# Stores whose tile ScalarE wrote last, issued from ScalarE's own transfer queue

## The chip, the cores and the metric

The kernel runs on one core of a Trainium2 chip. The metric is the device time of one execution in microseconds (us). The engines are TensorE (PE, with its weight loads as PEld), VectorE (DVE), ScalarE (ACT), GpSimd (POOL) and SyncE (SP); a "q" behind a name (SPq, ACTq) means the engine's sequencer, which waits and issues transfers.

## The reference

One layer of a streaming encoder with two parallel token mixers, on 2048 tokens of width 1024, in float32:

```
xn = RMSNorm(x)
[aq|ak|av|mq|mk|mv|mo|i|f|ga|gm] = xn @ w_in
A = chunked band attention (8 heads of 64, own chunk of 64 + 8 before, learned position bias)
M = mLSTM matrix memory (4 heads of 128, chunkwise; causal conv on q/k; headwise RMSNorm; sigmoid(mo))
y = sigmoid(ga) * (A @ w_att_proj) + sigmoid(gm) * (M @ w_mlstm_proj)
x = x + y @ w_out
x = x + relu(RMSNorm(x) @ w_up)^2 @ w_down
out = RMSNorm(x)
```

## The kernel before, in words

**Data.** The tokens are four blocks (b = 0 to 3) of 512. A tile is 128 partitions by 512 columns of float32 (256 KB). On-chip memory holds small pools of such tiles: 16 `ctx`, 6 `temp` (named tmp in the profile), 4 `sc`, 28 `r` (two halves each), 4 `wraw` and 3 `wsp` for weights, and 8 PSUM banks. Everything that is needed later is stored to DRAM and loaded again: gates (`gate`), conv outputs and output gates (`mfar`), values (`vspill`, `mvfar`), keys and queries (`kfar`, `qfar`), the ungated feed-forward activations (`u`), partial sums (`park`), combined weights (`wsum`).

**Products.** A float32 product is done as three passes over a high and a low half: ScalarE casts a tile to the high half, VectorE subtracts for the low half (weights: `split_now`, L501 and L503; operands: `split`, L1109 and L1114, L1111 and L1116), and PE runs high x high, high x low, low x high. Large products are done on 2 x 2 blocks with seven block products instead of eight (`quad`, L631; `product`, L662), so sums of blocks are made by VectorE and stored or split. `copied` (L1790) and `summed` (L1798) take results out of PSUM on ScalarE and VectorE.

**Stages.** In order: values for blocks 0 and 1; the input products (gates through tanh at L1930, the output gate `mo` scaled again at L1936); input products of blocks 2 and 3 with attention and recurrence of blocks 0 and 1 woven between; the projections of the mixers; the output product; the feed-forward up product, whose result is made relu (L2119) and square (L2123) by ScalarE; the down product, for the first half with attention and recurrence of blocks 2 and 3 woven in; the second half's out, up and down; the final norm.

**The order.** The program is written out by a planner, `Flow`. Every piece of work is a generator, a thread, that asks for an engine with a time (`yield "act", ns`), for a tile of a pool, or waits for an event. `Flow.run` always takes the request with the earliest planned start, advances the planned clock of that engine, and lets the thread emit its instructions. `fl.now` is the planned time of the running thread and the engine that set it. A request may hold two numbers: the first books the engine, the second is added for the thread alone. A transfer is a request for "sp": 800 ns of booked time for 256 KB, 1570 ns for 512 KB, and 2000 ns until it has landed. PE takes instructions in the order that the planner chose.

**Transfers.** All transfers but five are issued by SP. The five of ScalarE are a 12 KB load at the start (L308) and four stores of the output at the end (`turned_put`, L2316). Most stores go through one helper, `store`, L2041, whose issue is L2043. It is called by `sum_w` (weights), `park_u2` and `park_v`, `merge` (with the queue "sp!"), `evac_v` and `evac_mv` (values; the latter's writer is ScalarE at L1567), `gates_kept` and `gates_rest` (ScalarE at L1391 and L1521), `take_x1`, `keep` (the seven blocks of `u`), `after_vm`, `parts` (queries and keys: one half written by ScalarE at L1907, the other by VectorE at L1909), `after_in` (gates), `conv_far`, `x2_tile`, `norm_mid`, `final_keep` and `table`. For `u`, `sums` sends the blocks a11 and a12 directly when their square is done, and a22 and a21 behind VectorE steps:

```
yield "wait", [evs["a11"]]
a11 = tiles["a11"][:, :512]
send(0, a11)
```

Of the kernel before, what the change touches and what calls it, by code (L numbers as in the profile page):

```python
# [101 lines left out]
class Flow:  # L102
# [10 lines left out]
               act=dict(pe=220.0, act=130.0, dve=130.0, pool=180.0),  # L113
               dve=dict(pe=220.0, act=130.0, dve=130.0, pool=155.0), pool=dict(pe=290.0, act=130.0, dve=60.0),
               sp=dict())
# [132 lines left out]
class Layer:  # L248
# [1790 lines left out]
        fl.put(self.ctx, x)  # L2039

    def store(self, dst, src, ev, pool=None, item=None, queue="sp"):  # L2041
        yield queue, 800, 2000
        self.nc.sync.dma_start(dst, src)  # L2043
        self.fl.set(ev)
        if pool is not None:
            self.fl.put(pool, item)
# [517 lines left out]
```

## Time and profile before

| | |
|---|---|
| time, median of 3 runs | 2753.01 us (2751.06 to 2756.75) |
| profiled execution, its own time | 2753.07 us |
| its span | 2751.3 us |
| instructions | 38074 |
| granted PE clock | 0.998 |
| DMA: bytes, mean rate | 673.57 MB, 245 GB/s |
| issued from SP's queue (q1) | 670.08 MB |
| issued from ScalarE's queue (q10) | 1.06 MB |

The profile shows one execution. Busy times are unions of an engine's instructions; a matmul's end is modelled, so a busy PE is one that has work, not one at its peak. "Idle before, releaser" tells how long an engine was empty ahead of an instruction and what ended that. A wait in SP's queue is time in which the queue's head waited, and all transfers behind it.

### The profile page before, as it was taken

The numbers are of one execution on the slowest core, as the hardware profiler recorded it, in microseconds if no ns is written. First come the engines' busy times: TensorE is split into PE (matmuls) and PEld (weight loads), VectorE is DVE, ScalarE is ACT, GpSimd is POOL, SyncE is SP. The second block draws the span as 40 slices with busy tenths as digits, with TensorE's granted clock in tenths as the row PEclk, the third lists the DMA queues.
The fourth block names the chain that finished last, engine by engine and source line by source line (L and its number), as shares of the span: only waits on it lengthen the run. The fifth ranks groups of instructions, "written<-read, shape, count | busy, mean of one in ns | idle before, by whom it ended". The sixth has DMA issues, their size and how long they took to land.

```text
span 2751.3 us, 38074 instructions
## 1 busy us (share of the span) xinstructions
PE 2724.6 (99%) x12832; PEld 2261.5 (82%) x12832; DVE 2086.0 (76%) x3689; ACT 1526.4 (55%) x2640; POOL 44.6 (2%) x79
## 2 busy tenths in 40 slices
PE   9999999999999999999999999999999999999998
PEld 8878888788888887888888888888888888888887
DVE  7878776888775778897768889888888665667675
ACT  6545446666652434566556766657345565554443
POOL 0000000000000000000000000000000000000000
PEclk9999999999999999999999999999999999999999
DMA  8877678878877888767668778776864454588863
GB/s 295 284 254 268 234 267 281 260 235 266 255 256 254 299 305 294 244 212 260 246 237 295 254 231 223 239 257 199 294 227 171 151 205 154 180 278 281 283 230 137
DMA packets 331992, 673.57 MB, mean 245 GB/s; under 512 B 36900, under 2 KB 66468, under 8 KB 331796
## 3 DMA queue, kind: packets, MB, share of 16 engines
q1 hardware_dynamic: 331076, 670.08, 72.3%
q8 instruction: 101, 1.65, 0.2%
q10 hardware_dynamic: 720, 1.06, 0.1%
q14 instruction: 95, 0.78, 0.1%
HBM read 458.79 MB, written 212.21 MB: 244 GB/s over the span
## 4 chain that ended last, share of the span: by engine, by line
PE 83%; DVE 7%; DMA 4%; issue 3%; ACT 2%; POOL 0%; SPq 0%; POOLq 0%; DVEq 0%; ACTq 0%
PE bank L631 35%; PE bank L662 9%; PE bank L562 9%; PE bank L564 8%; PE bank L563 8%; PE bank L667 2%; PE bank L1337 2%; PE bank L1262 2%; PE bank L1369 2%; DVE wsp L503 1%; PE bank L856 1%; DVE r L1114 1%; DMA yp<-tmp 1%; DMA r<-u 1%; DVE ctx L1765 1%
## 5 line engine op out<-in xcount | busy, mean ns | idle before, releaser
L631 PE MATMUL bank<-r,wsp 128*128 128x512 f32 x4872 | 1110.9, 390 | 4.2 <-ACT r L1109 1.4
L631 PEld LDWEIGHTS bank<-r,wsp 128*128 128x128 f32 x4872 | 912.5, 188 | 198.2 <-ACT r L1109 2.1
L501 ACT CAST wsp<-wraw 128x1024 fp32r<-128x1024 f32 x439 | 461.3, 1051 | 492.1 <-PE bank L631 183.3
L503 DVE TENSOR_TENSOR wsp<-wraw,wsp 128x1024 fp32r<-128x1024 f32 x439 | 537.0, 1223 | 247.0 <-ACT wsp L501 236.7
L562 PE MATMUL bank<-r,wsp 128*128 128x512 f32 x1088 | 429.9, 396 | 0.3 <-DVE scs L1343 0.3
L564 PE MATMUL bank<-r,wsp 128*128 128x512 f32 x1088 | 425.3, 391 | 0.0
L563 PE MATMUL bank<-r,wsp 128*128 128x512 f32 x1088 | 425.2, 391 | 0.0
L662 PE MATMUL bank<-r,wsp 128*128 128x512 f32 x1512 | 370.8, 394 | 3.1 <-DVE ctx L780 2.5
L662 PEld LDWEIGHTS bank<-r,wsp 128*128 128x128 f32 x1512 | 279.4, 189 | 59.4 <-issue 2.7
L564 PEld LDWEIGHTS bank<-r,wsp 128*128 128x128 f32 x1088 | 204.3, 188 | 43.0
L562 PEld LDWEIGHTS bank<-r,wsp 128*128 128x128 f32 x1088 | 204.5, 188 | 38.4 <-DVE scs L1343 0.7
L563 PEld LDWEIGHTS bank<-r,wsp 128*128 128x128 f32 x1088 | 204.7, 188 | 38.1
L1114 DVE TENSOR_TENSOR r<-r 128x512 fp32r<-128x512 f32 x273 | 181.8, 687 | 56.8 <-ACT r L1109 55.0
L1109 ACT CAST r<-r 128x512 fp32r<-128x512 f32 x273 | 164.7, 621 | 104.4 <-DMA r<-u 77.1
L1798 DVE TENSOR_TENSOR ctx<-bank,ctx 128x512 f32<-128x512 f32 x150 | 103.0, 687 | 64.7 <-PE bank L631 63.6
L520 DVE TENSOR_TENSOR wraw<-wraw,wraw 128x1024 f32<-128x1024 f32 x112 | 136.5, 1220 | 2.2 <-DMA wsum<-wraw 1.0
L1350 ACT ACTIVATE sc<-sc,scs 128x640 f32<-128x640 f32 (+4 forms) x128 | 97.2, 760 | 54.9 <-DVE scs L1343 54.3
L1790 ACT COPY ctx<-bank 128x512 f32<-128x512 f32 x150 | 87.2, 581 | 52.0 <-PE bank L631 50.5
L2119 ACT ACTIVATE ctx<-ctx 128x512 f32<-128x512 f32 x96 | 60.5, 630 | 97.8 <-DVE ctx L1798 97.8
L1374 DVE TENSOR_TENSOR r<-bank,r 128x512 fp32r<-128x512 f32 (+1 forms) x168 | 96.4, 595 | 8.4 <-ACT r L1372 7.5
L1262 PE MATMUL bank<-r,r 128*128 128x512 f32 x336 | 95.7, 367 | 3.5 <-DVE ctx L1674 1.9
L1372 ACT CAST r<-bank 128x512 fp32r<-128x512 f32 (+1 forms) x168 | 80.7, 514 | 27.9 <-PE bank L1369 27.4
(257 smaller groups left out, 3054.1 us busy)
## 6 DMA issues: line engine op xcount, KB each, us to landing
wraw<-in_wf SPq DMA_DIRECT2D x196, 512.0 KB, 4.2
r<-u SPq DMA_DIRECT2D x224, 256.0 KB, 4.4
wraw<-wsum SPq DMA_DIRECT2D x104, 512.0 KB, 4.5
u<-ctx SPq DMA_DIRECT2D x128, 256.0 KB, 2.8
u<-tmp SPq DMA_DIRECT2D x96, 256.0 KB, 2.1
wraw<-in_w SPq DMA_DIRECT2D x47, 512.0 KB, 4.5
ctx<-in_wf SPq DMA_DIRECT2D x88, 256.0 KB, 4.2
wsum<-ctx SPq DMA_DIRECT2D x88, 256.0 KB, 3.1
```

The lines of the kernel that those rows point to most:

```text
L501: nc.scalar.copy(w[:, 0], raw)
L503: nc.vector.tensor_sub(w[:, 1], raw, w[:, 0].bitcast(F32))
L520: V.tensor_sub(dst, x, y)
L562: mm(ps, lh, rh, start=first, stop=False)
L563: mm(ps, lh, rl, start=False, stop=False)
L564: mm(ps, ll, rh, start=False, stop=last)
L631: mm(ps, wv[:, x, k, n], a[:, y], start=new and k == 0 and x == y == 0, stop=k == 3 and x == 1, skip_group_check=True)
L662: mm(ps, wv[:, x, k, n], a[:, y], start=start and x == y == 0, stop=stop and x == 1, skip_group_check=True)
L1109: self.nc.scalar.copy(dst[:, 0], src)
L1114: self.nc.vector.tensor_sub(dst[:, 1], src, dst[:, 0].bitcast(F32))
L1262: nc.tensor.matmul(bkv[:, :, c0:c0 + w], st, sl[:, :, o:o + w], start=n == 0, stop=n == total - 1)
L1798: nc.vector.tensor_add(t[:, o:o + 512], ps, t[:, o:o + 512])
```

## The change

`store` looks at which engine set its thread's planned time. If the queue was left at its default and that engine is ScalarE, the transfer is issued by ScalarE, as an instruction in ScalarE's own stream: 300 ns of planned waiting for the thread, then 60 ns of booked ScalarE time and 2800 ns until it has landed; SP's planned clock is not touched. In all other cases the helper does what it did. The planner runs over the whole program as before, so that all later choices of order are made with the changed clocks.

```
     def store(self, dst, src, ev, pool=None, item=None, queue="sp"):
-        yield queue, 800, 2000
-        self.nc.sync.dma_start(dst, src)
+        if queue == "sp" and self.fl.now[1] == "act":
+            yield "act", 0, 300
+            yield "act", 60, 2800
+            self.nc.scalar.dma_start(dst, src)
+        else:
+            yield queue, 800, 2000
+            self.nc.sync.dma_start(dst, src)
         self.fl.set(ev)
         if pool is not None:
             self.fl.put(pool, item)
```

## The prediction

> **What bounds the kernel now.** I read the page's busy times and chain first, then the table by stages, then the transfer queue's own waits, then single places.
>
> ```profile
> PE 2724.6 (99%) x12832; PEld 2261.5 (82%) x12832; DVE 2086.0 (76%) x3689; ACT 1526.4 (55%) x2640; POOL 44.6 (2%) x79
> ...
> PE 83%; DVE 7%; DMA 4%; issue 3%; ACT 2%; POOL 0%; SPq 0%; POOLq 0%; DVEq 0%; ACTq 0%
> ```
>
> TensorE (PE) is busy for 2724.6 of 2751.3 us, and the chain that ended last runs over it for 83%. ScalarE (ACT) has 2751.3 - 1526.4 = 1225 us without work. The sequencers that issue transfers (SPq, ACTq) hold 0% of the chain: what the change moves is not what the end waits for. The profiled execution took 2753.07 us, 1.8 us more than its span and 0.06 us from the median of 2753.01, so I add my terms to 2753.
>
> Where PE is idle shows in the table by stages (stretch, its length, busy time of each engine with its instructions, granted clock, share and rate of the DMA engines):
>
> ```profile
> core 0: us, PE busy (x) PEld busy (x) DVE busy (x) ACT busy (x) POOL busy (x), PEclk, DMA share, GB/s
> 0.00:100.00 100.00, 98.07 (x446) 81.80 (x447) 80.49 (x137) 62.63 (x98) 2.68 (x6) 1.00 0.86 304
> ...
> 250.00:450.00 200.00, 200.00 (x888) 165.71 (x888) 148.41 (x200) 103.55 (x151) 2.37 (x5) 1.00 0.73 264
> 450.00:600.00 150.00, 146.67 (x797) 122.63 (x796) 115.89 (x318) 101.53 (x253) 6.36 (x13) 1.00 0.83 258
> 600.00:750.00 150.00, 147.84 (x810) 126.10 (x809) 125.08 (x348) 100.09 (x218) 6.75 (x12) 0.99 0.82 259
> ...
> 1000.00:1060.00 60.00, 57.68 (x255) 47.45 (x254) 34.69 (x50) 17.27 (x25) 0.00 (x0) 1.00 0.85 294
> ...
> 1300.00:1480.00 180.00, 180.00 (x798) 148.97 (x797) 127.54 (x178) 96.31 (x142) 0.30 (x2) 1.00 0.71 248
> 1480.00:1700.00 220.00, 217.49 (x1167) 183.15 (x1166) 190.22 (x468) 159.20 (x337) 9.36 (x17) 1.00 0.78 249
> 1700.00:2000.00 300.00, 297.49 (x1518) 250.43 (x1517) 251.32 (x563) 168.43 (x332) 7.58 (x13) 1.00 0.77 247
> ...
> 2700.00:2752.00 52.00, 43.93 (x210) 36.53 (x208) 25.34 (x39) 18.39 (x31) 3.19 (x5) 0.95 0.32 119
> sum 2752.00, PE 2724.62 PEld 2261.46 DVE 2085.96 ACT 1526.37 POOL 44.61; mean PE 151.37 PEld 125.64 DVE 115.89 ACT 84.80 POOL 2.48
> ```
>
> PE is idle for 2751.3 - 2724.6 = 26.7 us in all. The start (1.93) and the tail (8.07, of which 0.7 lies behind the span's end) are outside the change's reach, which leaves 17.4 us. In the stages of pure products (250 to 450, 1300 to 1480), where many of the stores concerned lie, it is idle for nothing at all. The idle time is in the mixed stages, where attention and the recurrence are woven between products: 3.33 + 2.16 us between 450 and 750, 2.51 + 2.51 between 1480 and 2000, and 2.32 between 1000 and 1060, where the DMA engines are 85% busy.
>
> **What the change moves.** By the code, a store moves when the planner's clock of its thread was last set by ScalarE:
>
> ```profile
> u<-ctx SPq DMA_DIRECT2D x128, 256.0 KB, 2.8
> gate<-ctx SPq DMA_DIRECT2D x64, 256.0 KB, 3.0
> mfar<-ctx SPq DMA_DIRECT2D x48, 256.0 KB, 3.9
> mvfar<-tmp SPq DMA_DIRECT2D x8, 256.0 KB, 3.8
> gatepart<-tmp SPq DMA_DIRECT2D x1, 80.0 KB
> mrow<-tmp SPq DMA_DIRECT2D x4, 8.0 KB
> ```
>
> That is half of the u<-ctx (the quadrants a11 and a12, sent straight from the square's event; a21 and a22 are sent behind a VectorE step), all 64 gate<-ctx, the third of mfar<-ctx that is the output gate (L1936), and the last three rows: 64 + 64 + 16 + 8 + 1 + 4 = 157 of the transfers. The bytes stay as they are.
>
> **Taken off SP.** This is what the SP queue waited for, in total, times, longest:
>
> ```profile
> SPq L456 <- DVE wsp L503: 229.5, 114, 10.0
> ...
> SPq L2043 <- ACT ctx L2123: 152.7, 80, 9.6
> ...
> SPq L2043 <- ACT ctx L1930: 60.6, 43, 4.5
> ...
> SPq L2043 <- ACT tmp L1907: 30.3, 24, 3.0
> ...
> SPq L769 <- DMA mfar<-ctx: 6.7, 3, 3.6
> ```
>
> SP stands at the head of its line for ScalarE's squares (152.7 us) and gates (60.6 us), and all loads behind stand with it. With the 157 gone, those behind can go earlier. The stores themselves gain nothing: SP is already there when ScalarE ends. What it is worth is bounded from above by the PE idle time above, 17.4 us, since nothing else is in the end's way. The L1907 row, stores of a half that ScalarE wrote while VectorE set the clock, stays. The last row matters for the waits: a load of a parked tile stood for the landing of a store of another tensor, so an issue can wait for transfers a few places ahead of it, whoever issued them. I take a gain of 0 for this term, since the next thing that SP stands for, the weight slots of L503 (229.5 us), stays and holds the same loads.
>
> **Put on ScalarE.** The kernel's tail already has four such issues; these rows are one of them among its neighbours:
>
> ```profile
> 2738.86 0.73 ACT L2308 ACTIVATE sc<-sc,r_z 128x512 f32<-128x512 f32 x1 [0.85 <-POOL r_z L2291]
> 2739.49 0.71 ACT L2308 ACTIVATE ctx<-ctx,r_z 128x512 f32<-128x512 f32 x1
> 2739.62 0.35 ACTq L2316 DMA_DIRECT2D out_x<-sc  x1
> 2740.11 0.58 ACT L2298 ACTIVATE tmp<-bank 128x512 f32<-128x512 f32 x1
> ```
>
> The issue takes 0.35 us from the moment its tile is written (2738.86 + 0.73 = 2739.59), under the next operation (2739.49 to 2740.20); the one after starts at 2740.11, so nothing is lost. 157 x 0.35 = 55 us of ScalarE's sequencer. With an operation between, the cost is 0; directly behind its writer an issue leaves ScalarE empty for about 0.03 + 0.35 us, up to 60 us in all, against 1225 us that are free. The 300 ns which the planner puts ahead of the issue let the next operation go first, so I take 0. If that cover is gone, the wait is for what stands behind on ScalarE: the casts of the weights (L501), the copies that clear PSUM banks (L1790), the splits (L1109). The weight cast has a margin:
>
> ```profile
> L501 ACT CAST wsp<-wraw 128x1024 fp32r<-128x1024 f32 x439 | 461.3, 1051 | 492.1 <-PE bank L631 183.3 <-PE bank L563 170.6 <-issue 40.6
> ```
>
> It waits for PE to give back its slot, not the other way round. What a long stand of ScalarE costs PE is shown once in this trace:
>
> ```profile
> 1053.47 0.63 ACT L1111 ACTIVATE r<-tmp 128x512 fp32r<-128x512 f32 x1 [7.02 <-DMA tmp<-yp]
> ...
> 1058.25 3.92 PE L662 MATMUL bank<-r,wsp 128*128 128x512 f32 x16 [2.32 <-DVE ctx L780]
> ```
>
> ScalarE stood for 7.02 us for a late load; its next operations, then VectorE, were late by as much, and PE lost 2.32 us. So a stand up to about 4.7 us is covered, and 0.4 us per store is far inside it. Issue cost on the path: 0, between 0 and the price in the third rival.
>
> **What the new plan does.** The queue is also an entry of the planner's clocks: each store books 800 ns of SP. 157 x 0.8 = 126 us of booked transfer time vanish from its view, though the bytes still pass through the same engines, 83 to 86% busy in the stages at 0, 450 and 1000 us. From the first moved store on the greedy order is drawn anew, with loads expected sooner than they come: the plan lets a load land 2.8 us after its booking, while this one took
>
> ```profile
> r<-qfar SPq DMA_DIRECT2D x64, 256.0 KB, 5.7
> ```
>
> PE runs in its written order, so each place where the plan put attention's or the recurrence's matmuls too early is a stall of the kind at 1058 us. The cost can be below zero too: a redrawn order may lose less than the 12.8 us of the mixed and loaded stages. I take three more stalls of 2.32 us, because fewer booked transfers err in one direction, too early: 3 x 2.32 = +7 us.
>
> Sum: 2753 + 0 (SP freed) + 0 (issues) + 7 (order) = 2760 us.
>
> **Weighed against the skill.** SP's issues take 0% of the chain, as shown. The Trainium skill (DMA: Bandwidth & Descriptors, Issuing engines are not separate DMA queues) says that transfers started by several engines run on the same 16 DMA engines and that issuing from several saves only the sequencer's time; the trace agrees with it, and by it alone the time would stay 2753. The same page (Queues, rings and completion order) says that each DMA engine takes turns between queues, packet by packet; no run here shows it, and it would let a moved store pass loads that stand in SP's queue, which speaks against the change.
>
> **The rivals.**
> First, no change: the 157 stores are off any path before and after, and the new order loses as much as the old: 2753. For it: 0 us of idle PE in the pure stages. Against it: a redrawn order hardly falls on the same 17 us. That fewer stores move than I count ends here too.
>
> Second, faster: SP no longer stands for ScalarE, loads in the loaded stages come in time. If half of the 12.8 us of idle time between 450 and 750, 1000 and 1060, 1480 and 2000 goes, 2753 - 6.4 = 2746.6; if all of the 17.4 goes, 2735.6. For it: 213 us of such waits in two rows. Against: SP's larger wait stays.
>
> Third, much slower: ScalarE's issues wait for earlier transfers, in the way the L769 row shows SP doing it. Where SP is behind, the tile is ready and ScalarE stands, with the casts and bank copies behind it. Its place is the entry to the mixed stages, where the queue is in a burst (SP's issues in order of time, and the times of all transfers of the gate tensors):
>
> ```profile
> 1468.62 0.42 SPq L2043 DMA_DIRECT2D u<-ctx  x1
> ...
> 1474.38 6.55 SPq L2103 DMA_DIRECT2D r<-u  x7
> ```
>
> ```profile
> DMA to landing us min/median/max: 2.0/3.5/7.1
> ```
>
> It decides where the wait passes the cover of 4.7 us: with the 7.1 us of the slowest of these, 2.4 us each. At eight such places it is 19 us: 2772.
>
> **How the numbers follow.** 0.2% (5.5 us) is about what a measurement of this kernel can tell from no change. Forecast, 2760: 0.40. Third rival, 2772: 0.09. First rival, 2753: 0.24. Second, 2746.6 and below: 0.27. So slower 0.49, same 0.24, faster 0.27. The likeliest case's own range goes from two to six stalls, 2758 to 2767. The range over all: down to 2741, some 12 of the 17.4 us gone, and up to 2780, eleven places of the third rival's kind (26 us); about 2 in 10 lie outside.
>
> **What would show it.** Right: 157 + 5 issues on ACTq of about 0.35 us; the L2123, L1930 and L1936 rows of SP's waits shrink; PE idle still near zero in the pure stages, and some 7 us more of it in the mixed ones, ended by late loads or by VectorE behind them. The page's PE busy time should hardly move. First rival: idle time spread as now. Second: less than 5 us idle in 450 to 750 and 1480 to 2000 together. Third: ScalarE idle for 5 us and more ahead of L501 or L1790 with a transfer as what ended it, and PE idle behind. I am wrong if the pure stages gain or lose more than 3 us, for then the issues themselves have a price or a worth that I put at 0.

## The result

The changed kernel takes 2764.94 us (median of 6 runs, 2762.24 to 2767.75), the kernel before 2754.65 us beside it (6 runs, 2751.06 to 2758.56). The ratio is 1.0037, with a 95% interval of 1.0024 to 1.0051: slower by some 10 us. The profiled execution took 2762.7 us, its span is 2760.9 us.

The page's busy times and chain of the changed kernel:

```profile
PE 2724.1 (99%) x12832; PEld 2261.9 (82%) x12832; DVE 2082.2 (75%) x3696; ACT 1530.4 (55%) x2639; POOL 47.4 (2%) x79
...
PE 59%; DVE 6%; DMA 5%; ACT 2%; issue 2%; SPq 0%; POOL 0%; POOLq 0%; DVEq 0%; ACTq 0%
```

PE does the same work (2724.1 us against 2724.6); its idle time went from 26.7 to 2760.9 - 2724.1 = 36.8 us. In these two executions that is the whole difference. The table by stages says where (stretch, length, busy time of each engine, clock, DMA share and rate):

```profile
250.00:450.00 200.00, 199.15 (x883) 164.72 (x882) 146.95 (x197) 101.97 (x148) 1.69 (x5) 1.00 0.75 267
450.00:600.00 150.00, 146.24 (x808) 123.89 (x807) 114.84 (x329) 107.50 (x262) 6.27 (x14) 1.00 0.88 264
600.00:750.00 150.00, 147.20 (x802) 125.34 (x801) 126.09 (x348) 96.23 (x208) 7.65 (x11) 0.99 0.77 242
750.00:900.00 150.00, 148.47 (x696) 123.37 (x695) 98.15 (x161) 60.78 (x106) 2.08 (x3) 1.00 0.78 256
...
1060.00:1120.00 60.00, 57.92 (x252) 47.05 (x253) 56.54 (x85) 37.04 (x53) 0.00 (x0) 1.00 0.83 289
...
1300.00:1480.00 180.00, 180.00 (x798) 148.92 (x797) 128.97 (x179) 97.43 (x142) 0.11 (x1) 1.00 0.72 248
1480.00:1700.00 220.00, 214.74 (x1149) 182.00 (x1148) 184.12 (x462) 155.30 (x329) 9.40 (x18) 1.00 0.79 246
1700.00:2000.00 300.00, 296.09 (x1514) 247.88 (x1513) 251.30 (x571) 173.11 (x340) 9.51 (x13) 1.00 0.78 243
2000.00:2200.00 200.00, 200.00 (x884) 165.55 (x883) 159.33 (x209) 105.46 (x155) 0.00 (x0) 1.00 0.55 183
2200.00:2400.00 200.00, 197.94 (x874) 163.58 (x873) 123.40 (x145) 113.48 (x169) 0.00 (x0) 1.00 0.49 169
```

The mixed stages lose 3.76 + 2.80 us between 450 and 750 (5.49 before) and 5.26 + 3.91 between 1480 and 2000 (5.02 before). Two stages of pure products, which had nearly nothing, now lose 0.85 (250 to 450) and 2.06 us (2200 to 2400). The rest is spread in pieces of 1 to 2 us, and a few stages lose less than before.

What moved is what the prediction counted, 157 transfers, by the DMA issues:

```profile
gate<-ctx ACTq DMA_DIRECT2D x64, 256.0 KB, 4.1
u<-ctx ACTq DMA_DIRECT2D x64, 256.0 KB, 2.3
u<-ctx SPq DMA_DIRECT2D x64, 256.0 KB, 2.1
...
mfar<-ctx ACTq DMA_DIRECT2D x16, 256.0 KB, 3.2
...
mvfar<-tmp ACTq DMA_DIRECT2D x8, 256.0 KB, 4.1
...
gatepart<-tmp ACTq DMA_DIRECT2D x1, 80.0 KB
...
mrow<-tmp ACTq DMA_DIRECT2D x4, 8.0 KB
```

SP's own waits after (who waited for whom, total, times, longest; five lines were added to the file, so L2123 is now L2128 and the issue L2048):

```profile
SPq L456 <- DVE wsp L503: 270.8, 122, 8.7
SPq L447 <- DVE wsp L503: 178.9, 67, 8.6
SPq L2048 <- ACT ctx L2128: 111.9, 30, 8.2
...
SPq L447 <- DVE wraw L520: 50.0, 17, 10.8
...
SPq L769 <- DMA gate<-ctx: 27.8, 10, 5.9
```

The gates' waits (60.6 us) have no row left, those for the squares fell from 152.7 to 111.9 us. The first row, loads of weights that stand for their slot, rose from 229.5 to 270.8: SP's next head of line holds the same queue. The last row is a wait that the move makes longer: loads of parked tiles (L769) stand until a gate's store has landed. Before, it was

```profile
SPq L769 <- DMA gate<-ctx: 3.7, 3, 2.2
```

### The profile page after: what moved, and what is told of

Read it like the earlier page. It is cut to its first block, busy times and chain, and to the rows that moved or that the text cites. A ratio compares the mean times of both kernels' runs of the same rounds, so it can differ in the third digit from the quotient of the medians.

```text
span 2760.9 us, 38024 instructions
## 1 busy us (share of the span) xinstructions
PE 2724.1 (99%) x12832; PEld 2261.9 (82%) x12832; DVE 2082.2 (75%) x3696; ACT 1530.4 (55%) x2639; POOL 47.4 (2%) x79
## 4 chain that ended last, share of the span: by engine, by line
PE 59%; DVE 6%; DMA 5%; ACT 2%; issue 2%; SPq 0%; POOL 0%; POOLq 0%; DVEq 0%; ACTq 0%
PE bank L631 24%; PE bank L562 7%; PE bank L563 7%; PE bank L564 7%; PE bank L662 5%; PE bank L667 2%; PE bank L856 1%; PE bank L1262 1%; PE bank L1369 1%; DVE wsp L503 1%; PE bank L1337 1%; DMA r<-u 1%; DMA yp<-tmp 1%; DMA r<-mix 1%; DVE r L1114 0%
## 5 line engine op out<-in xcount | busy, mean ns | idle before, releaser
L503 DVE TENSOR_TENSOR wsp<-wraw,wsp 128x1024 fp32r<-128x1024 f32 x439 | 535.5, 1220 | 240.0 <-ACT wsp L501 236.2
L520 DVE TENSOR_TENSOR wraw<-wraw,wraw 128x1024 f32<-128x1024 f32 x112 | 136.3, 1218 | 1.5 <-DMA wsum<-wraw 0.4
L2124 ACT ACTIVATE ctx<-ctx 128x512 f32<-128x512 f32 x96 | 60.6, 631 | 95.2 <-DVE ctx L1798 77.8
L1337 PE MATMUL bank<-r,r 128*128 128x256 f32 (+2 forms) x464 | 88.6, 311 | 4.5 <-DMA r<-qfar 3.0
```

The source lines that it names most:

```text
L503: nc.vector.tensor_sub(w[:, 1], raw, w[:, 0].bitcast(F32))
L520: V.tensor_sub(dst, x, y)
L1337: nc.tensor.matmul(bk[:, :c1 - c0], q[:, y, i * P:(i + 1) * P], kf[:, f * P + c0:f * P + c1], start=y == 0, stop=y == 1)
```

## The experiments

Three theories. A: the plan loses, because booked transfer time vanished from it. B: the issue itself loses, by ScalarE's time or by leaving SP's queue. C: any redrawn order loses, the one of before was a good draw. All ratios are to the kernel before, run on the same chip. I also compared the written orders of PE's matmuls (12510 in the program, by source line and buffers), since a redraw shows there in thousands.

### Plan and issue apart

The plan of before, the issue by ScalarE (PE's order stays all but the same: 155 matmuls differ, against 9014 for the changed kernel):

```
+        last = queue == "sp" and self.fl.now[1] == "act"
         yield queue, 800, 2000
-        self.nc.sync.dma_start(dst, src)
+        (self.nc.scalar if last else self.nc.sync).dma_start(dst, src)
```

> The order of before is kept (the helper still books 800 ns of SP and waits for SP's clock), and the same stores are issued by ScalarE. Theory A (the redrawn order costs, because booked transfer time vanished): about 2754, within 4 us of before, PE idle in the stages as before. Theory B (the issues on ScalarE or the second queue cost): about 2765, idle PE as in the changed kernel. Theory C (any redrawn order loses more than the one of before): 2754, as A.

Measured: 2761.7 us, ratio 1.0036 (1.0023 to 1.0050). As slow as the changed kernel, with hardly any change of PE's order. That speaks for B, and shows that a loss of this size needs neither A nor C. Its profiled execution has a span of 2763.3 us, 12.0 us more than before: 7.0 us of that are idle time of PE, 5.0 us are busy time (2729.6 against 2724.6 us).

The plan of the change, the issue by SP (106 matmuls differ from the changed kernel's order):

```
             yield "act", 60, 2800
-            self.nc.scalar.dma_start(dst, src)
+            self.nc.sync.dma_start(dst, src)
```

> The plan of the changed kernel, all bookings as there, but the transfers are issued by SP. A: about 2765, idle PE in the mixed stages as in the changed kernel. B: about 2754. C: about 2765. If SP's standing for ScalarE matters, it comes out some us above the changed kernel.

Measured: 2770.23 us, ratio 1.0062 (1.0048 to 1.0075), the slowest of all. A plan that does not book SP while SP still does the work does lose, as theory A says; its idle PE time in the stage at 450 us is 7.13 us:

```profile
450.00:600.00 150.00, 142.87 (x772) 118.42 (x773) 111.93 (x312) 103.28 (x252) 7.06 (x13) 1.00 0.85 253
```

But within this plan the issue by ScalarE is the better one (1.0037 against 1.0062): here leaving SP's queue is worth some 7 us. Plan and issue are not two sums: each order is best with the queue that it was planned for.

The changed kernel with SP's booking put back:

```
             yield "act", 0, 300
+            self.fl.clock["sp"] += 800
             yield "act", 60, 2800
```

> The changed kernel, but each moved store also books 800 ns on SP's planned clock, so no transfer time vanishes from the planner's view. A: most of the loss is given back, 2754 to 2759. B: 2765. C: another order, anywhere from 2756 to 2775, with no tendency towards before.

Measured: 2761.18 us, ratio 1.0033 (1.0020 to 1.0046). The booking gives nothing back that can be told from the changed kernel's 1.0037. A's reason, the missing booking, falls for the change as it is. The order is also drawn anew here: 9867 matmuls differ from the changed kernel's.

### Redraws

The plan of before, with the landing time of a store changed by 100 ns either way. PE's order differs from before in 8378 and 8328 matmuls, nearly as much as the change makes:

```
-        yield queue, 800, 2000
+        yield queue, 800, 2100
```

> The kernel before, with one planned number in the store helper changed: a store is taken to land after 2100 ns and not 2000. No transfer moves to another queue and no booking vanishes, but the greedy order is drawn anew. A: 2754, within 4 us of before. B: 2754. C: slower than before by 4 to 15 us, idle PE again in the mixed stages but at other places.

Measured: 2751.42 us, ratio 0.9996 (0.9986 to 1.0006).

> A second redraw of the order of before: a store is taken to land after 1900 ns and not 2000, nothing else. If any redraw can lose as the changed kernel does (C), 2756 to 2770. If the loss comes from what the change does to the plan or to the queues (A, B), 2749 to 2756, like the redraw with 2100.

Measured: 2759.64 us, ratio 1.0015 (1.0006 to 1.0024). That lies in the band that I had named for theory C, with less than half of the changed kernel's loss.

The changed kernel, its moved stores planned to land after 2900 ns instead of 2800:

> A redraw of the changed kernel's order: its moved stores are taken to land after 2900 ns and not 2800. If the changed kernel was merely an unlucky draw (C), it lies anywhere between 2750 and 2770. If the move costs whatever the draw (A, B), 2760 to 2770.

Measured: 2766.44 us, ratio 1.0039 (1.0026 to 1.0052). This is hardly a new draw, though: by source line PE's order is the changed kernel's, and 2009 matmuls differ in their buffers alone. Real new draws of the changed plan are the kernel with SP's booking put back (1.0033) and the one with a longer wait at the end of this section (5383 matmuls differ, 1.0034). So a new order is worth between nothing and 4 us in two draws of the old plan, and the changed plan loses some 9 us in two draws of its own. As the whole cause C falls. It leaves a warning: a difference of 0.15% can come from the order alone.

Two things set the five kernels with the changed plan, its variants and redraws included, apart from the nine with the old one, whoever issues in them. Between 1480 and 2000 us their PE is idle for 6.4 to 9.3 us (the changed kernel: 9.17); with the old plan and its redraws it is 3.5 to 5.9 us. The kernel with the old plan and ScalarE's issue loses 2.42 + 3.10 us there:

```profile
1480.00:1700.00 220.00, 217.58 (x1160) 182.62 (x1159) 185.87 (x466) 156.59 (x332) 11.11 (x18) 1.00 0.81 252
1700.00:2000.00 300.00, 296.90 (x1520) 249.46 (x1518) 253.07 (x569) 169.67 (x337) 8.80 (x13) 1.00 0.77 245
```

The other is PE's granted clock, which is listed as a mean for every execution. None of the 32 executions with the changed plan has more than 0.998, and the changed kernel's mean is 0.9972. The kernel before, beside the experiments, has 0.999 or more in 53 of 77 executions (mean 0.9988), the old plan with ScalarE's issue has 0.9987, the two redraws 0.9986 and 0.9987. In those 77 executions the time falls with the clock: on the three chips they took 2756.1, 2756.9 and 2755.6 us on average at 0.998, and 2752.3, 2753.8 and 2753.5 us at 0.999. My estimate from these numbers is 2 to 4 us for a thousandth, so that 3 to 6 of the changed kernel's 10 us would go with its clock. The two profiled executions compared above are both at 0.998 and do not show this part. Why the changed order runs at a lower clock is open; being slow is not enough, since the old plan with ScalarE's issue is as slow without it.

### The issue, taken apart

ScalarE's time without any issue: SP issues all stores, and small squares are added beside each of the 157.

```
         self.nc.sync.dma_start(dst, src)
+        for _ in range(2 if last else 0):
+            self.nc.scalar.square(self.rr["z0"][:, :2], self.ones)
```

> The kernel before with its plan and with all stores issued by SP, and two squares of a 128 x 2 tile added on ScalarE beside each of the 157 stores, unknown to the planner: some 0.4 us of ScalarE time each, about what an issue takes there. If ScalarE's time is what the old plan with ScalarE's issues lost (B, engine), 2758 to 2764. If the second queue, or the order in which transfers go, is what lost (B, queue), 2750 to 2756.

Measured: 2757.04 us, ratio 1.0010 (1.0002 to 1.0019), between the two expectations.

> Three times the added ScalarE time: plan and issues of before, six squares of a 128 x 2 tile beside each of the 157 stores, some 125 us more of ScalarE. With two it was 1.0010. If ScalarE's time is what costs, 1.003 or more. If ScalarE has room for it, as I predicted for the issues, 1.001 again.

Measured: 2758.89 us, ratio 1.0014 (1.0006 to 1.0023). The groups by line of the two kernels, with six and with two squares:

```profile
L2046 ACT ACTIVATE r_z<-ones 128x2 f32<-128x2 f32 x942 | 188.4, 200 | 19.0
```

```profile
L2046 ACT ACTIVATE r_z<-ones 128x2 f32<-128x2 f32 x314 | 62.5, 199 | 4.4
```

Three times the time, 188.4 us against 62.5, costs 0.04% more, less than the intervals tell apart. ScalarE has room.

The stores off SP, but on GpSimd's queue, with ScalarE left alone:

```
-        self.nc.sync.dma_start(dst, src)
+        (self.nc.gpsimd if last else self.nc.sync).dma_start(dst, src)
```

> The plan of before, and the 157 stores issued from GpSimd's queue, so that they leave SP's queue without taking anything of ScalarE. If ScalarE's time is the cost (B, engine), 2749 to 2756. If leaving SP's queue is the cost (B, queue), 2759 to 2768. GpSimd's own way of issuing may add a cost that the profile of its rows would show.

Measured: 2759.73 us, ratio 1.0020 (1.0010 to 1.0030). That is at the lower edge of what I had named for leaving SP's queue, and its interval overlaps that of the redraw with 1900 ns. Nor is it free of GpSimd's own way of issuing: GpSimd is busy for 133.3 us here and for 44.6 us before, and no run separates what that costs. Its profile shows where SP's waits go. In the second up product, from 2130 to 2400 us, SP's waits before were

```profile
SPq L2043 <- ACT ctx L2123: 89.0, 41, 9.6
SPq L447 <- DVE wsp L503: 57.2, 15, 8.1
...
SPq L447 <- DVE wraw L520: 16.4, 6, 3.1
```

and with GpSimd's issue

```profile
SPq L447 <- DVE wsp L503: 78.5, 20, 8.6
SPq L2044 <- ACT ctx L2124: 66.3, 14, 8.2
SPq L447 <- DVE wraw L520: 27.1, 7, 10.7
```

The 22.7 us that SP no longer stands for squares come back as 21.3 + 10.7 us at weight slots. One PE stall in this stretch grows when the squares' stores leave SP in the old plan. Before, with GpSimd's issue, with ScalarE's issue in the old plan, and in the changed kernel (timelines, start and duration, the brackets give the idle time before):

```profile
2231.71 2.56 PE L631 MATMUL bank<-r,wsp 128*128 128x512 f32 x10 [0.48 <-DVE ctx L1798]
```

```profile
2235.77 10.53 PE L631 MATMUL bank<-r,wsp 128*128 128x512 f32 x39 [3.32 <-DVE ctx L1798]
```

```profile
2241.38 1.89 PE L631 MATMUL bank<-r,wsp 128*128 128x512 f32 x7 [1.72 <-DVE ctx L1798]
```

```profile
2240.94 1.43 PE L631 MATMUL bank<-r,wsp 128*128 128x512 f32 x5 [2.06 <-DVE ctx L1798]
```

The largest one, 3.32 us, is in the kernel in which ScalarE issues none of these stores, so here it is not the time of an issue on ScalarE. But this stall is not the price. It is 1.21 us with the six squares and 1.22 us with the changed plan and SP's issue, where no store has left SP. And the changed plan with a longer wait, below, loses as much as the changed kernel without any stall there:

```profile
2099.78 308.00 PE L631 MATMUL bank<-r,wsp 128*128 128x512 f32 x1357
```

Over the whole stretch from 2000 to 2700 us, PE's idle time is 0.59 us before, 4.01 us with GpSimd's issue, 3.70 us with ScalarE's issue in the old plan and 2.47 us in the changed kernel; it is 0.56 us in the changed plan with a longer wait.

The two families apart, in the plan of before:

```
-        last = queue == "sp" and self.fl.now[1] == "act"
+        last = queue == "sp" and self.fl.now[1] == "act" and pool is None
```

> The plan of before, and only the 64 stores of u go out from ScalarE; the other 93 stay on SP. The full move cost 1.0036 with this plan. If the price is per issue and the same everywhere, 64 of 157 of it: 1.0015. If it sits in the stages between 100 and 1110 us, where the DMA engines are over 80% busy in places, 1.000. If it sits in the up products, 1.003.

Measured: 2758.01 us, ratio 1.0010 (0.9999 to 1.0022).

> The counterpart: the plan of before, the gates, output gates, values and rows (93 stores) from ScalarE, the u stores from SP. Price per issue: 1.0021. All of it in the stages up to 1110 us: 1.0035. All of it in the up products: 1.000. The two halves should add up to about 1.0036.

Measured: 2760.23 us, ratio 1.0019 (1.0009 to 1.0030). Together 1.0029, against 1.0036 for all. Shares by count would be 1.0015 and 1.0021, and the runs agree with that, though the first cannot be told from no change. That one family carries the whole price, which would have taken 1.003 for the first or 1.0035 for the second, lies outside the intervals.

The changed kernel with a longer planned wait ahead of the issue:

```
-            yield "act", 0, 300
+            yield "act", 0, 900
```

> The changed kernel with 900 ns of planned waiting ahead of the issue instead of 300, so that more issues stand behind another operation of ScalarE and fewer directly in front of the next. If the issues that hold up the next operation are the price, 1.001 to 1.002 and fewer of them in the trace. If their place does not matter, 1.003 to 1.004 like the other redraws of the changed plan.

Measured: 2765.12 us, ratio 1.0034 (1.0022 to 1.0046). This one did not test what it was for. Counted in its trace, 66 issues still end less than 250 ns ahead of ScalarE's next operation, 69 in the changed kernel: the place of an issue in ScalarE's stream did not follow the planned wait. It stands as one more redraw of the changed plan, and gives the same time as the others. Its mean granted clock is 0.9974.

What one such issue looks like, directly behind its writer, in the kernel with the old plan (ScalarE's timeline):

```profile
2236.10 0.63 ACT L2124 ACTIVATE ctx<-ctx 128x512 f32<-128x512 f32 x1
2236.76 0.35 ACTq L2044 DMA_DIRECT2D u<-ctx  x1
2237.16 1.05 ACT L501 CAST wsp<-wraw 128x1024 fp32r<-128x1024 f32 x1 [0.42 <-PE bank L631]
```

and the same square and cast before:

```profile
2226.50 0.62 ACT L2123 ACTIVATE ctx<-ctx 128x512 f32<-128x512 f32 x1
2227.02 1.04 ACT L501 CAST wsp<-wraw 128x1024 fp32r<-128x1024 f32 x1
```

The cast starts 0.43 us after the square's end, where it started 0.10 us ahead of it: 0.53 us at this place. The bracket names PE for that gap; the issue ending at 2237.11 is what stands in it.

## Why the prediction was right and wrong

The time was forecast as +7 us and came out as +10.3 (2764.94 - 2754.65), inside the range and of the right sign. That the sum came so close is luck: two of its terms were wrong.

**The price of the move itself, put at 0 + 0, is the step that failed.** In the plan of before, with the order that PE had, moving the issue alone costs 1.0036, some 10 us. I costed it by ScalarE's time alone. That part was nearly right in size: ScalarE's time by itself costs 1.0010, and 1.0014 at three times the dose. (Its reason was not: the 300 ns did not keep the issues away from the next operation, as the 69 counted above show.) What I left out is that leaving SP's queue can have a price of its own. GpSimd's issue, which takes nothing of ScalarE, came out at 1.0020. I had listed "SP freed" with an upper bound of 17.4 us of gain and no lower bound. In the old plan it is on the other side of zero or at it; only in the changed plan is the move off SP a gain (1.0062 with SP's issue, 1.0037 with ScalarE's).

**Where SP stands next** was read rightly: weight slots. Their two rows for L503 rose from 229.5 + 153.5 to 270.8 + 178.9 us, the row of L520 for the same loads from 29.8 to 50.0; that is 87 us, while the rows for squares and gates lost 152.7 + 60.6 - 111.9 = 101 us. The stands for gates' stores to land (L769) add 27.8 - 3.7 = 24.1 us; they are 25.8 us in all with ScalarE's issue in the old plan and 33.3 us with GpSimd's. All rows together rose from 1753 to 1842 us, by more than the 157 x 0.32 = 50 us of issues that SP no longer has. So SP stands no less than before, only at other places. The step from there to "a value of 0" failed, but how these waits turn into idle time of PE is not shown: the stall near 2235 us is absent from a kernel with the same loss.

**The new order, put at +7, had a wrong reason, and its size is open.** With ScalarE's issue the old and the new plan give 1.0036 and 1.0037, as if the order were free, and the redraws of the old plan 0.9996 and 1.0015. It is not free: with SP's issue the new order costs 1.0062. In every kernel that has it PE loses more between 1480 and 2000 us, one of the mixed stages where I had put its stalls, and the granted clock is lower. So the two plans lose the same 10 us at least in part at different places; what the new order spares of the price that the move has in the old one is not shown. The reason "because fewer booked transfers err in one direction" failed: what it costs would have been given back by booking them, and was not (1.0033). The clock was not in the prediction at all.

**The rivals.** No change and faster are out by the interval. The third, ScalarE standing for earlier transfers, is in the traces, with a size that makes it harmless. In the changed kernel an issue waits for 0.9 us at most with ScalarE empty. The longest stand is in the old plan with ScalarE's issue, where three issues take 3.57 us:

```profile
954.64 3.57 ACTq L2044 DMA_DIRECT2D gate<-ctx  x3
958.26 0.63 ACT L1930 ACTIVATE ctx<-ctx 128x512 f32<-128x512 f32 x1 [3.88 <-DMA mfar<-ctx]
```

That is below the cover of 4.7 us from which I said it decides, and PE is busy through it. One row of ScalarE's waits looks like the rival and is not:

```profile
ACT ctx L2124 <- DMA u<-ctx: 17.0, 9, 1.9
```

One of its nine places, with VectorE's sum, and the same place before:

```profile
1258.09 0.33 ACTq L2045 DMA_DIRECT2D u<-ctx  x1
1259.22 0.68 DVE L1798 TENSOR_TENSOR ctx<-bank,ctx 128x512 f32<-128x512 f32 x1
1259.94 0.63 ACT L2124 ACTIVATE ctx<-ctx 128x512 f32<-128x512 f32 x1 [1.89 <-DMA u<-ctx]
```

```profile
1256.37 0.63 ACT L2119 ACTIVATE ctx<-ctx 128x512 f32<-128x512 f32 x1 [1.89 <-DVE ctx L1798]
```

The relu starts 0.04 us after the sum has ended, at this place as at the other eight, and the gap is 1.89 us with and without the issue: it is a wait for VectorE, put down to a transfer. **The signs.** 157 issues: right. ScalarE's rows in SP's waits shrink: right. PE's busy time unmoved: right for the changed kernel (5.0 us more in the old plan with ScalarE's issue). Idle time mostly in the mixed stages: right. The pure stages were to stay near zero: they gained 0.85 us at 250 to 450 and 2.06 - 0.48 = 1.6 us at 2200 to 2400. That is 2.4 us, just inside the 3 us that I named, but it is not where the price sits: the changed plan with a longer wait has 0 idle time in both stages and loses as much.

**The rule that I weighed.** I used the rule of the Trainium skill (DMA: Bandwidth & Descriptors, Issuing engines are not separate DMA queues) for the rival of no change. That nothing is lost by issuing from another engine, which I read into it, the runs do not bear out: 1.0036 in the old plan. That only the sequencer's time is saved, they neither show nor refute: the move is a gain of some 7 us in the changed plan, where SP's queue is planned without these stores.

**What stays open.** Single shares of 0.1 to 0.2% are no larger than a redraw's, so 1.0010 for ScalarE's time and 1.0020 for leaving SP's queue are not shown to be the two parts of 1.0036. How leaving SP's queue turns into idle time of PE is not shown. Nor is it shown why the changed order runs at a lower clock, or why its losses and those of the move do not add up. No version that was run beats the kernel before; the nearest, the redraw with 2100 ns, is the same within its interval.

## What to carry to other kernels

When a transfer is moved to another queue in a program whose order is planned, run the two halves apart, the new plan with the old queue and the old plan with the new one: a total that agrees with the forecast can hide two wrong terms. Here, taking a wait out of the head of SP's queue moved the stand to the next head, and the sum of its waits did not fall. Look at the granted clock of all executions as well as at the profiled one: a part of a small loss can go with it. Before a wait is put down to a transfer, look for the same gap in the kernel before. Before a loss of 0.1 to 0.4% is explained by a mechanism, redraw the order once or twice with a number that should not matter, to see how much the order alone can do, and check that the order did change.

## What the runs showed of the hardware

An issue on ScalarE takes 0.33 us of its sequencer (the median of the 157), and directly behind its writer, at the place shown, it delays the next operation by 0.53 us. GpSimd's issue of the same store took 0.54 us:

```profile
2234.40 0.54 POOL L2044 DMA_DIRECT2D u<-ctx  x1 [1.80 <-ACT ctx L2124]
```

What I had not expected is how little ScalarE's time weighs in a kernel whose PE is busy for 99%: 188 us of added operations cost some 4 us (1.0014). And the time of one and the same kernel falls by 2 to 4 us from a granted clock of 0.998 to one of 0.999, by the 77 executions above.
